# Order of the seven products in a Strassen-like feed-forward, and where the last layer norm's first row tiles are worked

## The chip, the cores and the metric

One core of one Trainium2 chip. The metric is the device time of one execution in microseconds (us). TensorE (PE) multiplies, VectorE (DVE), ScalarE (ACT) and GpSimd (POOL) work element by element, and SyncE (SP) issues most transfers.

## The reference

Two layers over 512 tokens of width 1024, in float32. The first mixes tokens with a state-space model, the second with attention. After each mixer and after each feed-forward part the sum with the input is normalised. The change touches the second layer's feed-forward and its norm, the last thing that is computed:

```python
def sq_relu_mlp(h, w1, w2):                       # w1 1024x4096, w2 4096x1024
    return jnp.square(jax.nn.relu(h @ w1)) @ w2

def layer_norm(x, g, b):
    mu = jnp.mean(x, axis=-1, keepdims=True)
    var = jnp.mean(jnp.square(x - mu), axis=-1, keepdims=True)
    return (x - mu) * lax.rsqrt(var + LN_EPS) * g + b

h = layer_norm(DN_ALPHA * h + sq_relu_mlp(h, w_ff1[1], w_ff2[1]), ln_ffn_g[1], ln_ffn_b[1])
```

## The kernel before

**Float32 as two parts.** Each operand of a matmul is cut into a rounded part and a remainder (`hi` and `lo`, float32r), and a product is three matmuls: hi x hi, lo x hi, hi x lo. For activations and weights alike ACT rounds (a copy into `hi`) and DVE subtracts (`lo`). In tile names `fh`, `fl` are the parts of hidden activations, `whi`, `wlo` those of a weight block.

**Weight blocks.** `ahead` loads 1 MB blocks in a fixed order on SP's queue into two `raw` buffers and splits them into three pairs of `whi`/`wlo` (L541 ACT, L543 DVE, the latter in two halves). A load waits until the split two blocks earlier has freed its buffer; block k + 3 is loaded as block k's product begins, and block k + 2 is split after the first half of product k.

**The last feed-forward, `feed_forward_rows`.** It runs in four quarters q of 1024 hidden units. A quarter first forms its hidden units in eight blocks of 128 units x 512 tokens (`dense`, L608 to L610; the first quarter has one weight unit of the four here, the rest earlier), then multiplies them with its part of `w2`. Two blocks form a pair, handled by `Pairs.add`: ACT takes relu and square into `sq`. With a block p and then q, cut into token halves, the second multiplication is done as a two by two scheme of seven products instead of eight (Strassen's, in a form with the sums p - q, `inner`, and `one`, made for the four pairs of a quarter). DVE forms these sums, and for each ACT rounds and DVE subtracts. `fo` holds the two parts of `one`, which only product 1 reads. Products 3 and 4 read a block itself (`hi[0]`, first and second half), 2 and 5 the difference `out`, 6 and 7 `in`.

**The products.** `SEVEN` lists in which order they are done and to which parts of the result each is added. One product is 24 matmuls: two row halves t = 0, 1, four pairs each, three matmuls (L886 to L888) per pair. The result stays in SBUF as row tiles 0 to 3 of 128 tokens x 1024, each as two `z` tiles of 128x512; DVE adds each product to them from PSUM (L976). A product's entry (r, n, sign) stands for row tile 2r + t and column half n. Row tiles 0 and 1 get additions from products 1, 3, 4, 5 and 7 only; products 2 and 6 go to row tiles 2 and 3 alone.

`w2` is combined in the same way: a block is plain, or the sum of two (16 such sums are made ahead in DRAM by a copy on SP's queue and an adding DMA on GpSimd's, L566 and L568), or a difference. A difference is loaded as two blocks and subtracted by DVE (L555) before it is split. `BLOCKS` lists this per product, in the order of `SEVEN`.

**The end.** In the last quarter products 2 and 6 are done for t = 0 first and then for t = 1. `norm(t)` works on DVE with one square root on ACT: two `bn_stats`, the root's reciprocal, then for each half a subtraction of the mean with the scale `g` (L923, L930) and a multiply-add with `b` into `o` (L932), stored by SP (L933). The norms of row tiles 0 and 1 run after product 2 of t = 0, that of tile 2 after product 2 of t = 1, that of tile 3 at the end. All order within `feed_forward_rows` is as written (a manual schedule); each engine runs its instructions in that order.

Of the kernel before, what the change touches and what calls it, by code (L numbers as in the profile page):

```python
# [9 lines left out]
F32 = mybir.dt.float32  # L10
F32R = mybir.dt.float32r
I32 = mybir.dt.int32
AF = mybir.ActivationFunctionType
ALU = mybir.AluOpType
# [3 lines left out]
DM = 1024  # L18
# [58 lines left out]
class Net:  # L77
# [590 lines left out]
    class Norm:  # L668
# [43 lines left out]
        def root(self):  # L712
            next(self.r)
# [130 lines left out]
    class Pairs:  # L844
# [4 lines left out]
        def add(self, ps):  # L849
            net, nc, v = self.net, self.net.nc, self.net.nc.vector  # L850
            first, second = slice(0, T // 2), slice(T // 2, T)
            x = net.f("sq")
            nc.scalar.activation(x, ps, AF.Relu)
            nc.scalar.activation(x, x, AF.Square)
            if self.p is None:
                self.p = x
                self.hi, self.lo = [[net.f(n, dt=F32R) for _ in range(3)] for n in ("fh", "fl")]
                self.one = net.f("fo", dt=F32R)
                self.inner = net.f("in")
                v.tensor_tensor(self.inner[:, first], x[:, second], x[:, first], op=ALU.subtract)  # L860
                nc.scalar.copy(self.hi[0][:, first], x[:, first])
                v.tensor_tensor(self.lo[0][:, first], x[:, first], self.hi[0][:, first].bitcast(F32), op=ALU.subtract)
                return
            p, q, hi, lo, one, inner = self.p, x, self.hi, self.lo, self.one, self.inner
            self.p = self.inner = None
            outer = net.f("out")
            v.tensor_tensor(outer, p, q, op=ALU.subtract)
            nc.scalar.copy(hi[1], outer)
            v.tensor_tensor(inner[:, second], q[:, first], q[:, second], op=ALU.subtract)
            nc.scalar.copy(hi[2], inner)  # L870
            v.tensor_tensor(p[:, first], p[:, first], q[:, second], op=ALU.subtract)
            nc.scalar.copy(one[:, first], p[:, first])
            nc.scalar.copy(hi[0][:, second], q[:, second])
            v.tensor_tensor(lo[1], outer, hi[1].bitcast(F32), op=ALU.subtract)
            v.tensor_tensor(lo[2], inner, hi[2].bitcast(F32), op=ALU.subtract)
            v.tensor_tensor(one[:, second], p[:, first], one[:, first].bitcast(F32), op=ALU.subtract)
            v.tensor_tensor(lo[0][:, second], q[:, second], hi[0][:, second].bitcast(F32), op=ALU.subtract)
            cut = lambda i, c: (hi[i][:, c], lo[i][:, c])
            self.out.append({1: (one[:, first], one[:, second]), 2: cut(1, second), 3: cut(0, first), 4: cut(0, second),
                             5: cut(1, first), 6: cut(2, first), 7: cut(2, second)})  # L880

    def mm3_rows(self, ps, a, tok, w, k, start, stop):
# [5 lines left out]
        pe.matmul(ps, ahi[:, tok], wlo[:, k, :], start=False, stop=stop)  # L888


    SEVEN = ((1, ((0, 0, 1), (1, 1, 1))), (3, ((0, 1, 1), (1, 1, 1))), (7, ((0, 0, 1),)), (4, ((0, 0, 1), (1, 0, 1))),
             (5, ((0, 0, 1), (0, 1, -1))), (2, ((1, 0, 1), (1, 1, -1))), (6, ((1, 1, 1),)))

    def feed_forward_rows(self, u0, h, act, pairs, rows, out):

        nc, v, pe = self.nc, self.nc.vector, self.nc.tensor
        toks = [slice(128 * t, 128 * t + 128) for t in range(4)]
        z = [[None, None] for _ in toks]
        g, b = [], []
# [9 lines left out]
                    nc.scalar.mul(z[t][n], ps, ALPHA)  # L909
                    yield  # L910

        def norm(t):

            self.n += 1
            st = self.small.tile([128, 16], F32, tag="st", name=f"st{self.n}")
            mu, var, s, y, r = [st[:, i:i + 1] for i in (12, 13, 14, 15, 0)]
            yield v.bn_stats(st[:, 0:6], z[t][0])
            v.bn_stats(st[:, 6:12], z[t][1])
            v.bn_aggr(st[:, 12:14], st[:, 0:12])
            v.tensor_scalar(var, var, self.col(6), None, op0=ALU.add)  # L920
            nc.scalar.activation(s, var, AF.Sqrt)
            v.reciprocal(y, var)
            v.scalar_tensor_tensor(z[t][0], z[t][0], mu, g[0], op0=ALU.subtract, op1=ALU.mult)  # L923

            v.scalar_tensor_tensor(y, s, 0.5, y, op0=ALU.mult, op1=ALU.mult)
            v.reciprocal(r, s)
            v.scalar_tensor_tensor(y, r, 0.5, y, op0=ALU.mult, op1=ALU.add)
            for n in range(2):
                if n:
                    v.scalar_tensor_tensor(z[t][n], z[t][n], mu, g[n], op0=ALU.subtract, op1=ALU.mult)  # L930
                o = self.f("o")
                v.scalar_tensor_tensor(o, z[t][n], y, b[n], op0=ALU.mult, op1=ALU.add)  # L932
                nc.sync.dma_start(out=out[toks[t], 512 * n:512 * n + 512], in_=o)  # L933

        N, first = 11, 4

        def start(i):
            self.ahead(u0 + i + 4, 0)

        def middle(i):  # L940
            self.ahead(0, u0 + i + 3)

        with self.tc.manual_schedule():
            turn = turned()
            self.ahead(0, u0 + 5)
            for q in range(4):
                last = q == 3
# [13 lines left out]
                if last:  # L961
                    for i, x in enumerate((g, b)):
                        for n in range(2):
                            x.append(self.f("gb", pool=self.B))
                            nc.sync.dma_start(out=x[n], in_=rows[i:i + 1, 512 * n:512 * n + 512].to_broadcast([128, 512]))
                left, todo, ws = pairs.out, [], {}
                pairs.out = []

# [8 lines left out]

                for i, (m, outs) in enumerate(self.SEVEN[0:5 if last else 7]):
                    at = N * q + first + i
                    start(at)  # L980
                    ws[m] = self.split_t.pop(u0 + at)
                    for t in range(2):
                        product(m, t, outs)
                        if t == 0:
                            middle(at)
                        if last and m == 5:
                            todo.append(norm(t))
            self.n += 1
            pre = self.small.tile([128, 1], F32, tag="pre", name=f"pre{self.n}")
            nc.scalar.activation(pre, left[0][3][0][:, 0:1].bitcast(F32), AF.Sqrt, bias=self.col(6), scale=0.0)  # L990
            for m in (2, 6):
                ws[m] = self.split_t.pop(u0 + 3 * N + first + (5 if m == 2 else 6))
            for t in range(2):
                for m, outs in self.SEVEN[5:7]:
                    product(m, t, outs)
                    if m == 2:
                        for c in todo:
                            for _ in c:
                                pass
                        todo = [norm(2 + t)]  # L1000
                        next(todo[0])
            for _ in todo[0]:
                pass

    def boundary(self, u, src, settle, z, g, b, follow, pool=None, begun=None):

# [411 lines left out]
FILL = {26: 4, 29: 2, 30: 4, 31: 1, 33: 1, 35: 2}  # L1418
UNITS = dict(glu=8, w_out=4, ff0=32, kvq=3, att=8, wo=4)

BLOCKS = ((0, 3, ALU.subtract), (1, 3, ALU.add), (2, 3, ALU.add), (2, 0, ALU.add), (3,), (0,), (0, 1, ALU.add))


@with_exitstack
def net_kernel(ctx, tc, a):
# [14 lines left out]
    for q in range(4):  # L1440
        for i in range(11):
            src = [a["ff1"][8 * q + j].rearrange("p k n -> p (k n)") for j in range(8)]
            if i < 4:
                units.append((src[i], (8, 256), 0))
                continue
            c = BLOCKS[i - 4]
            if len(c) > 1 and c[2] == ALU.add:
# [126 lines left out]
```

## Time and profile before

| | |
|---|---|
| median of three runs | 1190.16 us (1188.77 to 1190.49) |
| profiled execution, its own time | 1187.36 us |
| its span, first to last instruction | 1185.6 us |
| TensorE busy | 1136.3 us, 96% |
| DVE, ACT, GpSimd busy | 66%, 47%, 2% |
| mean granted TensorE clock | 0.991 of full |

A share is an average over stages: what an edit is worth is read where it stands, from what the engine that sets the end waits for.

### The profile page before, as it was taken

The numbers are of one execution on the slowest core, as the hardware profiler recorded it, in microseconds if no ns is written. First come the engines' busy times: TensorE is split into PE (matmuls) and PEld (weight loads), VectorE is DVE, ScalarE is ACT, GpSimd is POOL, SyncE is SP. The second block draws the span as 40 slices with busy tenths as digits, with TensorE's granted clock in tenths as the row PEclk, the third lists the DMA queues.
The fourth block names the chain that finished last, engine by engine and source line by source line (L and its number), as shares of the span: only waits on it lengthen the run. The fifth ranks groups of instructions, "written<-read, shape, count | busy, mean of one in ns | idle before, by whom it ended". The sixth has DMA issues, their size and how long they took to land.

```text
span 1185.6 us, 15947 instructions
## 1 busy us (share of the span) xinstructions
PE 1136.3 (96%) x6384; PEld 972.7 (82%) x6384; DVE 787.2 (66%) x1397; ACT 558.5 (47%) x939; POOL 20.2 (2%) x30
## 2 busy tenths in 40 slices
PE   5899999999999999999999999999999999999993
PEld 3778788899888888888899779989978878878872
DVE  8999552477454433433576788868887676676688
ACT  4888551337413413313436666634773643643540
POOL 0000000000011101000000000000000000000000
PEclk9999999999999999999999999999999999999997
DMA  4123261223699999722321012221335344344431
GB/s 169 40 91 95 89 222 71 72 72 108 187 282 269 293 325 247 215 107 72 107 72 45 32 59 90 72 72 40 116 135 210 114 154 159 142 142 165 155 142 71
DMA packets 39722, 157.54 MB, mean 133 GB/s; under 512 B 11456, under 2 KB 11584, under 8 KB 26720
## 3 DMA queue, kind: packets, MB, share of 16 engines
q1 hardware_dynamic: 30048, 137.64, 32.2%
q0 software_dynamic: 8448, 16.78, 8.0%
q10 hardware_dynamic: 1152, 2.10, 0.5%
q8 instruction: 50, 0.82, 0.3%
q14 instruction: 24, 0.20, 0.1%
HBM read 152.31 MB, written 37.75 MB: 160 GB/s over the span
## 4 chain that ended last, share of the span: by engine, by line
PE 85%; DVE 10%; ACT 4%; issue 1%; DMA 0%
PE ps L610 21%; PE ps L609 21%; PE ps L608 21%; PE ps L887 4%; PE ps L888 4%; PE ps L886 4%; PE ps L397 1%; PE ps L396 1%; PE ps L315 1%; PE ps L380 1%; PE ps L1329 1%; PE ps L642 1%; PE ps L352 1%; DVE wlo L543 1%; DVE tmpw L264 1%
## 5 line engine op out<-in xcount | busy, mean ns | idle before, releaser
L541 ACT CAST whi<-raw 128x2048 fp32r<-128x2048 f32 (+1 forms) x99 | 181.8, 1843 | 173.5 <-DMA raw<-in_ff 112.3
L543 DVE TENSOR_TENSOR wlo<-raw,whi 128x1024 fp32r<-128x1024 f32 (+1 forms) x198 | 225.5, 1179 | 37.6 <-ACT whi L541 37.6
L608 PE MATMUL ps<-hh,whi 128*128 128x512 f32 (+1 forms) x704 | 244.6, 347 | 0.0
L609 PE MATMUL ps<-hl,whi 128*128 128x512 f32 (+1 forms) x704 | 243.4, 346 | 0.0
L610 PE MATMUL ps<-hh,wlo 128*128 128x512 f32 (+1 forms) x704 | 243.3, 346 | 0.0
L609 PEld LDWEIGHTS ps<-hl,whi 128*128 128x128 f32 x704 | 133.3, 189 | 16.3
L610 PEld LDWEIGHTS ps<-hh,wlo 128*128 128x128 f32 x704 | 133.3, 189 | 16.3
L608 PEld LDWEIGHTS ps<-hh,whi 128*128 128x128 f32 x704 | 133.3, 189 | 16.2
L608 PE MATMUL ps<-fh,whi 128*128 128x512 f32 (+1 forms) x304 | 108.4, 357 | 0.0
L609 PE MATMUL ps<-fl,whi 128*128 128x512 f32 (+1 forms) x304 | 108.1, 355 | 0.0
L610 PE MATMUL ps<-fh,wlo 128*128 128x512 f32 (+1 forms) x304 | 108.1, 355 | 0.0
L796 ACT ACTIVATE relu<-ps 128x512 f32<-128x512 f32 x32 | 19.0, 595 | 127.7 <-PE ps L610 127.7
L798 DVE TENSOR_TENSOR relu<-relu 128x512 f32<-128x512 f32 x32 | 22.1, 691 | 84.3 <-ACT fh L797 84.3
L976 DVE TENSOR_TENSOR z<-z,ps 128x512 f32<-128x512 f32 x96 | 62.0, 682 | 22.1 <-PE ps L888 21.7
L886 PE MATMUL ps<-whi,fh 128*128 128x512 f32 x192 | 74.7, 389 | 0.0
L888 PE MATMUL ps<-wlo,fh 128*128 128x512 f32 x192 | 74.7, 389 | 0.0
L887 PE MATMUL ps<-whi,fl 128*128 128x512 f32 x192 | 74.7, 389 | 0.0
L609 PEld LDWEIGHTS ps<-fl,whi 128*128 128x128 f32 x304 | 57.4, 189 | 8.2
L610 PEld LDWEIGHTS ps<-fh,wlo 128*128 128x128 f32 x304 | 57.4, 189 | 8.2
L608 PEld LDWEIGHTS ps<-fh,whi 128*128 128x128 f32 x304 | 57.4, 189 | 8.1
L814 DVE TENSOR_TENSOR z<-z,ps 128x512 f32<-128x512 f32 (+1 forms) x30 | 17.4, 579 | 55.8 <-PE ps L610 55.8
L608 PE MATMUL ps<-yh,whi 128*128 128x512 f32 x128 | 52.3, 410 | 0.0
(302 smaller groups left out, 2207.9 us busy)
## 6 DMA issues: line engine op xcount, KB each, us to landing
raw<-in_ff SPq DMA_DIRECT2D x64, 1024.0 KB, 4.8
sum<-in_ff POOLq DMA_DIRECT2D x16, 1024.0 KB, 13.3
raw<-sum SPq DMA_DIRECT2D x16, 1024.0 KB, 4.8
raw<-in_glu SPq DMA_DIRECT2D x8, 1024.0 KB, 5.7
raw<-in_w_out SPq DMA_DIRECT2D x4, 1024.0 KB, 4.8
raw<-in_wo SPq DMA_DIRECT2D x4, 1024.0 KB, 4.7
raw<-in_kvq SPq DMA_DIRECT2D x3, 1024.0 KB, 4.8
raw<-in_attq SPq DMA_DIRECT2D x4, 576.0 KB, 3.6
```

The source lines that it names most:

```text
L541: self.nc.scalar.copy(hi, raw)
L543: self.put_off(lambda c=c: self.nc.vector.tensor_tensor(lo[:, c], raw[:, c], hi[:, c].bitcast(F32), op=ALU.subtract))
L608: pe.matmul(ps, whi, ahi, start=start, stop=False)
L609: pe.matmul(ps, whi, alo, start=False, stop=False)
L610: pe.matmul(ps, wlo, ahi, start=False, stop=stop)
L796: self.nc.scalar.activation(r, ps, AF.Relu)
L798: self.nc.vector.tensor_tensor(r, r, r, op=ALU.mult)
L814: v.tensor_tensor(z[m][:, tok], z[m][:, tok], ps, op=ALU.add)
L886: pe.matmul(ps, ahi[:, tok], whi[:, k, :], start=start, stop=False)
L887: pe.matmul(ps, alo[:, tok], whi[:, k, :], start=False, stop=False)
L888: pe.matmul(ps, ahi[:, tok], wlo[:, k, :], start=False, stop=stop)
L976: v.tensor_tensor(x, x, ps, op=ALU.add if sign > 0 else ALU.subtract)
```

## The change

The seven products are done in the order 3, 4, 5, 7, 1, 2, 6 instead of 1, 3, 7, 4, 5, 2, 6, and the weight blocks follow, so that the difference (two loads) stands at place five instead of one. `Pairs.add` makes the second half of `hi[0]`, `lo[0]` first instead of last. In the last quarter row tiles 0 and 1 are complete after the fifth product, and their norms (`norm_early`) begin there: ACT takes sums, squares and the scaling, DVE the steps of one element per row; the factor `g` is multiplied by GpSimd for tile 0 and by DVE for tile 1. For tiles 0 to 2 the offset `b` is first written to `out` by one DMA of 384 rows, and the rest is added to it by DMAs of GpSimd's queue; tile 2's last scaling goes to ACT. Tile 3 is as before.

```diff
@@ Pairs.add
             outer = net.f("out")
+            nc.scalar.copy(hi[0][:, second], q[:, second])
             v.tensor_tensor(outer, p, q, op=ALU.subtract)
+            v.tensor_tensor(lo[0][:, second], q[:, second], hi[0][:, second].bitcast(F32), op=ALU.subtract)
             nc.scalar.copy(hi[1], outer)
...
             nc.scalar.copy(one[:, first], p[:, first])
-            nc.scalar.copy(hi[0][:, second], q[:, second])
...
             v.tensor_tensor(one[:, second], p[:, first], one[:, first].bitcast(F32), op=ALU.subtract)
-            v.tensor_tensor(lo[0][:, second], q[:, second], hi[0][:, second].bitcast(F32), op=ALU.subtract)
@@ order
-    SEVEN = ((1, ((0, 0, 1), (1, 1, 1))), (3, ((0, 1, 1), (1, 1, 1))), (7, ((0, 0, 1),)), (4, ((0, 0, 1), (1, 0, 1))),
-             (5, ((0, 0, 1), (0, 1, -1))), (2, ((1, 0, 1), (1, 1, -1))), (6, ((1, 1, 1),)))
+    SEVEN = ((3, ((0, 1, 1), (1, 1, 1))), (4, ((0, 0, 1), (1, 0, 1))), (5, ((0, 0, 1), (0, 1, -1))), (7, ((0, 0, 1),)),
+             (1, ((0, 0, 1), (1, 1, 1))), (2, ((1, 0, 1), (1, 1, -1))), (6, ((1, 1, 1),)))
-BLOCKS = ((0, 3, ALU.subtract), (1, 3, ALU.add), (2, 3, ALU.add), (2, 0, ALU.add), (3,), (0,), (0, 1, ALU.add))
+BLOCKS = ((1, 3, ALU.add), (2, 0, ALU.add), (3,), (2, 3, ALU.add), (0, 3, ALU.subtract), (0,), (0, 1, ALU.add))
@@ feed_forward_rows: the norms
+        def root(var, s, y, r):
             nc.scalar.activation(s, var, AF.Sqrt)
             v.reciprocal(y, var)
+            yield v.scalar_tensor_tensor(y, s, 0.5, y, op0=ALU.mult, op1=ALU.mult)
+            v.reciprocal(r, s)
+            v.scalar_tensor_tensor(y, r, 0.5, y, op0=ALU.mult, op1=ALU.add)
+        def norm_early(t):
+            st, (nm, var, s, y, r) = stats(t)
+            o = [self.f("o") for _ in range(2)]
+            for n in range(2):
+                nc.scalar.activation(o[n], z[t][n], AF.Identity, accum_out=st[:, 1 + n:2 + n])
+            yield
+            v.tensor_tensor(nm, st[:, 1:2], st[:, 2:3], op=ALU.add)
+            v.tensor_scalar(nm, nm, -1.0 / DM, None, op0=ALU.mult)
+            for n in range(2):
+                nc.scalar.activation(o[n], z[t][n], AF.Square, bias=nm, accum_out=st[:, 3 + n:4 + n])
+            yield
+            v.tensor_tensor(var, st[:, 3:4], st[:, 4:5], op=ALU.add)
+            v.tensor_scalar(var, var, 1.0 / DM, self.col(6), op0=ALU.mult, op1=ALU.add)
+            for _ in root(var, s, y, r):
+                pass
+            v.tensor_tensor(nm, nm, y, op=ALU.mult)
+            for n in range(2):
+                nc.scalar.activation(o[n], z[t][n], AF.Identity, bias=nm, scale=y)
+            yield
+            for n in range(2):
+                (nc.gpsimd if t == 0 else v).tensor_tensor(o[n], o[n], g[n], op=ALU.mult)
+                nc.gpsimd.dma_start(out=out[toks[t], 512 * n:512 * n + 512], in_=o[n], accum_op=ALU.add)
-        def norm(t):
+        def norm(t, late):
...
+            for _ in root(var, s, y, r):
+                v.scalar_tensor_tensor(z[t][0], z[t][0], mu, g[0], op0=ALU.subtract, op1=ALU.mult)
...
                 o = self.f("o")
+                if late:
+                    v.scalar_tensor_tensor(o, z[t][n], y, b[n], op0=ALU.mult, op1=ALU.add)
+                    nc.sync.dma_start(out=out[toks[t], 512 * n:512 * n + 512], in_=o)
+                else:
+                    nc.scalar.mul(o, z[t][n], y)
+                    nc.gpsimd.dma_start(out=out[toks[t], 512 * n:512 * n + 512], in_=o, accum_op=ALU.add)
@@ feed_forward_rows: the last quarter, after the loads of g and b
+                    nc.sync.dma_start(out=out[0:384, :], in_=rows[1:2, :].to_broadcast([384, DM]))
...
-                        if last and m == 5:
-                            todo.append(norm(t))
+                        if last and m == 1:
+                            todo.append(norm_early(t))
+                            for c in todo:
+                                next(c)
...
+            n0, n1 = todo
+            n2, n3 = norm(2, False), norm(3, True)
+            between = {(0, 2): (n0, n1), (0, 6): (n0, n1, n2), (1, 2): (n1, n2, n3), (1, 6): (n3,)}
             for t in range(2):
                 for m, outs in self.SEVEN[5:7]:
                     product(m, t, outs)
-                    if m == 2:
-                        for c in todo:
-                            for _ in c:
-                                pass
-                        todo = [norm(2 + t)]
-                        next(todo[0])
-            for _ in todo[0]:
-                pass
+                    for c in between[t, m]:
+                        next(c, None)
```

Three places of the programs. First TensorE at the start of the last quarter's products, right behind the hidden units. Before, the first two pairs of product 1:
```order
L886 MATMUL ps_9845<-whi_9701,fo_9522 128x512
L887 MATMUL ps_9845<-whi_9701,fo_9522 128x512
L888 MATMUL ps_9845<-wlo_9702,fo_9522 128x512
L886 MATMUL ps_9845<-whi_9701,fo_9610 128x512
L887 MATMUL ps_9845<-whi_9701,fo_9610 128x512
```
Now, the first two pairs of product 3:
```order
L886 MATMUL ps_9841<-whi_9699,fh_9516 128x512
L887 MATMUL ps_9841<-whi_9699,fl_9519 128x512
L888 MATMUL ps_9841<-wlo_9700,fh_9516 128x512
L886 MATMUL ps_9841<-whi_9699,fh_9602 128x512
L887 MATMUL ps_9841<-whi_9699,fl_9605 128x512
```
What stood on `fo` now stands on `fh` and `fl`, the first token halves of the blocks.

Second DVE after product 2 of t = 0 in the last quarter (line numbers grow by 35 or so in the changed kernel; `st` holds a row tile's statistics). Before, two additions to row tile 2, then the norm of tile 0 (`z_7932` and `z_8000`), of which the second half's passes and then all of tile 1's norm follow:
```order
L976 TENSOR_TENSOR z_7986<-z_7986,ps_10026 128x512
L976 TENSOR_TENSOR z_8014<-z_8014,ps_10026 128x512
L917 BN_STATS st_10041<-z_7932 128x6
L918 BN_STATS st_10041<-z_8000 128x6
L919 BN_AGGR st_10041<-st_10041 128x2
L920 TENSOR_SCALAR st_10041<-st_10041,c 128x1
L922 RECIPROCAL st_10041<-st_10041 128x1
L923 SCALAR_TENSOR_TENSOR z_7932<-z_7932,st_10041,gb_9835 128x512
L925 SCALAR_TENSOR_TENSOR st_10041<-st_10041 128x1
L926 RECIPROCAL st_10041<-st_10041 128x1
L927 SCALAR_TENSOR_TENSOR st_10041<-st_10041 128x1
L932 SCALAR_TENSOR_TENSOR o_10052<-z_7932,st_10041,gb_9839 128x512
```
Now:
```order
L1011 TENSOR_TENSOR z_7981<-z_7981,ps_10041 128x512
L1011 TENSOR_TENSOR z_8009<-z_8009,ps_10041 128x512
L937 TENSOR_TENSOR st_10010<-st_10010 128x1
L938 TENSOR_SCALAR st_10010<-st_10010,c 128x1
L920 RECIPROCAL st_10010<-st_10010 128x1
L921 SCALAR_TENSOR_TENSOR st_10010<-st_10010 128x1
L922 RECIPROCAL st_10010<-st_10010 128x1
L923 SCALAR_TENSOR_TENSOR st_10010<-st_10010 128x1
L941 TENSOR_TENSOR st_10010<-st_10010 128x1
L932 TENSOR_TENSOR st_10034<-st_10034 128x1
L933 TENSOR_SCALAR st_10034<-st_10034 128x1
```
The passes over 128x512 tiles are gone from between; steps of one element per row are left, each group behind ACT's passes.

Third ACT at the end, from the split of product 6's block on. Before, one square root for each of the four norms:
```order
L541 CAST whi_10004<-raw_9952 128x2048
L990 ACTIVATE pre_10024<-fh_9516,c 128x1
L921 ACTIVATE st_10041<-st_10041 128x1
L921 ACTIVATE st_10059<-st_10059 128x1
L921 ACTIVATE st_10077<-st_10077 128x1
L921 ACTIVATE st_10124<-st_10124 128x1
```
Now (the first dozen; tile 1's scaling, tile 2's root, two scalings of tile 2 and tile 3's root follow):
```order
L541 CAST whi_10005<-raw_9955 128x2048
L930 ACTIVATE o_10011,st_10010<-z_7927 128x512
L930 ACTIVATE o_10012,st_10010<-z_7995 128x512
L935 ACTIVATE o_10011,st_10010<-z_7927,st_10010 128x512
L935 ACTIVATE o_10012,st_10010<-z_7995,st_10010 128x512
L930 ACTIVATE o_10035,st_10034<-z_7934 128x512
L930 ACTIVATE o_10036,st_10034<-z_8002 128x512
L1027 ACTIVATE pre_10039<-fh_9516,c 128x1
L919 ACTIVATE st_10010<-st_10010 128x1
L943 ACTIVATE o_10011<-z_7927,st_10010 128x512
L943 ACTIVATE o_10012<-z_7995,st_10010 128x512
L935 ACTIVATE o_10035,st_10034<-z_7934,st_10034 128x512
```
Tile 0 is `o_10011` and `o_10012`, tile 1 `o_10035` and `o_10036`; L930 takes sums, L935 squares, L943 scales. The passes of the two tiles interleave, and the root of tile 0 stands behind the sums of tile 1.

On GpSimd, which had no instruction after 627 us, there now follow a library reload, and in the end two multiplications and six adding DMAs in the order of the tiles. On SP's queue the write of 384 rows of `out` stands behind the four loads of `g` and `b`, ahead of the load of the fourth product's block.

## Rows read from the trace of the kernel before

**Rows 1.** The page: busy us, share and instructions of each engine.
```profile
PE 1136.3 (96%) x6384; PEld 972.7 (82%) x6384; DVE 787.2 (66%) x1397; ACT 558.5 (47%) x939; POOL 20.2 (2%) x30
```

**Rows 2.** Timeline, last quarter's first product: start us, duration us, [idle before].
```profile
1125.60 0.39 PE L886 MATMUL ps<-whi,fo 128*128 128x512 f32 x1
1127.09 0.69 DVE L867 TENSOR_TENSOR out<-sq,sq 128x512 f32<-128x512 f32 x1 [0.83 <-ACT sq L854]
1128.86 0.40 ACT L872 CAST fo<-sq 128x256 fp32r<-128x256 f32 x1
1129.31 0.50 PE L886 MATMUL ps<-whi,fo 128*128 128x512 f32 x1 [1.52 <-ACT fo L872]
1133.45 0.39 PE L886 MATMUL ps<-whi,fh 128*128 128x512 f32 x1
```

**Rows 3.** Timeline: first matmuls of products one and two, quarters 1-3.
```profile
872.44 0.48 PE L886 MATMUL ps<-whi,fo 128*128 128x512 f32 x1
879.77 0.39 PE L886 MATMUL ps<-whi,fh 128*128 128x512 f32 x1
955.93 0.39 PE L886 MATMUL ps<-whi,fo 128*128 128x512 f32 x1
963.79 0.39 PE L886 MATMUL ps<-whi,fh 128*128 128x512 f32 x1
1039.95 0.39 PE L886 MATMUL ps<-whi,fo 128*128 128x512 f32 x1
1049.41 0.40 PE L886 MATMUL ps<-whi,fh 128*128 128x512 f32 x1
```

**Rows 4.** Windows, third quarter: busy PE PEld DVE ACT POOL, PEclk, DMA, GB/s.
```profile
1046.00:1048.00 2.00, 2.00 (x6) 1.59 (x5) 2.00 (x3) 0.00 (x0) 0.00 (x0) 0.51 0.00 0
```

**Rows 5.** Timeline of DVE over the norms at the end.
```profile
1158.13 1.29 DVE L976 TENSOR_TENSOR z<-z,ps 128x512 f32<-128x512 f32 x2 [0.69 <-PE ps L888]
1160.65 0.21 DVE L919 BATCH_NORM_AGGREGATE st<-st 128x2 f32<-128x12 f32 x1
1162.33 0.75 DVE L932 SCALAR_TENSOR_TENSOR o<-z,st,gb 128x512 f32<-128x512 f32 x1
1169.56 0.69 DVE L917 BATCH_NORM_STATS2 st<-z 128x6 f32<-128x512 f32 x1
1181.62 0.75 DVE L932 SCALAR_TENSOR_TENSOR o<-z,st,gb 128x512 f32<-128x512 f32 x1
```

**Rows 6.** Block loads: a pair's landing, DVE's subtraction, ACT's cast.
```profile
DMA to landing us min/median/max: 4.7/5.8/6.8
1111.55 2.36 DVE L555 TENSOR_TENSOR raw<-raw,raw 128x1024 f32<-128x1024 f32 x2
L541 ACT CAST whi<-raw 128x2048 fp32r<-128x2048 f32 (+1 forms) x99 | 181.8, 1843 | 173.5 <-DMA raw<-in_ff 112.3
```

**Rows 7.** Windows while `gb` loads move; DMA issues, DRAM copies.
```profile
1123.00:1124.00 1.00, 1.00 (x6) 0.82 (x5) 0.10 (x1) 0.86 (x1) 0.00 (x0) 1.00 0.95 367
1124.00:1125.00 1.00, 1.00 (x6) 0.83 (x5) 1.00 (x1) 0.00 (x0) 0.00 (x0) 1.00 0.09 35
sum<-in_ff SPq DMA_DIRECT2D x16, 9.5
```

**Rows 8.** Lines: ACT's square of 128x512, its accumulator's read.
```profile
L854 ACT ACTIVATE sq<-sq 128x512 f32<-128x512 f32 x32 | 20.2, 632 | 1.0
L1309 ACT ACTIVATION_READ_ACCUMULATOR p<-ps,sst 128x1 f32 x32 | 6.3, 196 | 0.0
```

**Rows 9.** GpSimd: lines; its DMA queue; adding DMAs, us to landing.
```profile
L242 POOL MEMSET TT<- 128x1024 f32 x2 | 1.8, 954 | 0.0
L568 POOL DMA_DIRECT2D sum<-in_ff x16 | 16.6, 1038 | 461.3 <-DMA sum<-in_ff 461.3
q0 software_dynamic: 8448, 16.78, 8.0%
sum<-in_ff POOLq DMA_DIRECT2D x16, 1024.0 KB, 13.3
```

More of the change, by code (lines that the diff above doesn't have):

```diff
@@ L910, in turned, with stats @@
                     yield
-        def norm(t):
+        def stats(t):
             self.n += 1
             st = self.small.tile([128, 16], F32, tag="st", name=f"st{self.n}")
-            mu, var, s, y, r = [st[:, i:i + 1] for i in (12, 13, 14, 15, 0)]
+            return st, [st[:, i:i + 1] for i in (12, 13, 14, 15, 0)]
+        def root(var, s, y, r):
+            nc.scalar.activation(s, var, AF.Sqrt)
+            v.reciprocal(y, var)
+            yield v.scalar_tensor_tensor(y, s, 0.5, y, op0=ALU.mult, op1=ALU.mult)
[24 more added lines that the diff above has]
+        def norm(t, late):
+            st, (mu, var, s, y, r) = stats(t)
             yield v.bn_stats(st[:, 0:6], z[t][0])
@@ L920, in norm @@
             v.tensor_scalar(var, var, self.col(6), None, op0=ALU.add)
[L921 to L927, printed above, removed]
+            for _ in root(var, s, y, r):
+                v.scalar_tensor_tensor(z[t][0], z[t][0], mu, g[0], op0=ALU.subtract, op1=ALU.mult)
             for n in range(2):
@@ L931, in norm @@
                 o = self.f("o")
-                v.scalar_tensor_tensor(o, z[t][n], y, b[n], op0=ALU.mult, op1=ALU.add)
-                nc.sync.dma_start(out=out[toks[t], 512 * n:512 * n + 512], in_=o)
+                if late:
[4 more added lines that the diff above has]
+                    nc.gpsimd.dma_start(out=out[toks[t], 512 * n:512 * n + 512], in_=o, accum_op=ALU.add)
         N, first = 11, 4
```

## Prediction

> **What bounds the kernel now.** The page comes first: TensorE is busy for 96% of the span [rows 1], so only two kinds of time can be won, gaps in its work and the time after its last matmul. I looked for the gaps with the waits of TensorE over the last layer: there are two waits at the start of each quarter's products and no other. The timeline of the last quarter shows why [rows 2]. Call the start of its products T = 0 (1125.60). Product 1 reads `fo`, the last thing that the last pair makes: the square is ready just before 1127.09, DVE forms `out`, `in` and p - q, ACT rounds two tiles, and `fo` only then, at 1128.86. TensorE, which has run nine matmuls on older pairs by then, waits 1.52 us for it, and a little more for DVE's remainder. The second product starts at 1133.45, 7.85 us after the first. Without a gap a product is 24 matmuls at about 0.227 us, 5.44 us, so this start costs 2.4 us. The same two rows for the other quarters [rows 3] give 7.33, 7.86 and 9.46 us: 1.9, 2.4 and 4.0 us lost. The third is dearer since the granted clock stands at 0.51 for some 3 us after the gap [rows 4], the level of 1.2 GHz: 6 matmuls in 2 us where the full clock gives 9.
>
> The end is bound by DVE. From 1158.13 (T+32.5) it has work without a pause to 1182.37 (T+56.8) [rows 5], long after TensorE's last matmul. The span ends 3.2 us after DVE, with the last output transfer.
>
> **The starts.** Product 3, now first, reads the first token halves of `fh` and `fl`, made when the first block of each pair came, 5 us earlier. Product 4, due at T+5.44, reads the second halves. In the new `add` ACT rounds them first: square ready at T+1.45, copy 0.40, DVE's `out` to 2.1, `fl` at T+2.5: 2.9 us to spare. Products 5 and 7 need tiles that exist by T+4.3 and start at T+10.9 and T+16.3; `fo` has until T+21.8. No start should wait. Gain in the first three quarters: 1.9 + 2.4 + 4.0 = 8.3 us. The 2.4 us of the last are inside the end's sum, below.
>
> **The weights.** The block made of two loads and a DVE subtraction moves from position one of a quarter, where DVE had the slack of the matmuls on `act`, to position five. In the last quarter I laid the DVE and transfer rows end to end: pair work to T+4.6, two updates (0.6 each, [rows 5]) to 5.8, the split of product 5's block to 8.1, at 2.36 for a DVE pass over a block [rows 6]. That frees the buffer for the two loads; a pair lands 4.7 and 6.8 us after issue [rows 6], T+15. The subtraction, ACT's casts and the remainders, two such passes, are done at about T+20.4, and product 1 wants them from T+21.8: 1.4 us to spare. DVE is late by then with three updates, and the block of product 6 is loaded at T+20.4, lands 4.7 us later, is cast in 1.84 [rows 6] by 27.1 and split by 29.5, its first half by 28.3; the matmul that reads that half stands at T+30.4. So the chain stays hidden, by 1.4 to 2 us. If that cover is gone, each us of it is a us of time.
>
> **The prefill of `out`.** 1.5 MB from DRAM to DRAM, put on SP's queue behind the four `gb` loads. Those fill the DMA engines to T-1 and then leave them [rows 7]. The `gb` rows are the nearest: broadcast lines of the same tensor, 367 GB/s. By them it takes 4.3 us, 5.3 with some loss, and is over by T+4.5. Behind it waits only the load of product 7's block, 1 MB, which then lands by about T+8, when ACT asks for it (the middle of product 4, T+8.2). Price zero. The other bound is the row of DRAM copies, 9.5 us for 1 MB [rows 7], 14 us for this one: then that load lands at about T+16.5, when its product is due at 16.3. Its cast and split make TensorE wait and the two loads behind it wait too; laid out the same way it moves the end by 6 us. Those 9.5 us were measured amid other loads and adding DMAs; I take 4.3 to 5.3, as the tensor and the broadcast are the same.
>
> **The norms.** DVE loses the two norms of row tiles 0 and 1 and the last multiply-add of tile 2. ACT gets, for each of the two, four passes with accumulation or a square (0.63 [rows 8], 0.53 from one to the next, and 0.20 for the accumulator's read [rows 8]) and two scalings. In order:
> DVE ends the split at T+29.5 and updates tiles 1 and 3 to 30.8; tile 0's mean is at 31.1. ACT: its squares 31.2 to 32.7, tile 1's sums to 34.2, the early `Sqrt`, tile 0's root at 34.5, its scaling to 36.4, tile 1's squares to 37.8. DVE waits for ACT here, 3.4 us in three pieces. Tile 1's root takes it from 37.9 to 39.1 (the steps of one element are 0.08 to 0.25 us apart; all those of a norm fill 1160.65 to 1162.33 less one 0.67 us pass [rows 5]). From there DVE has no pause. Tiles 2 and 3 took it from 1169.56 to 1182.37, 12.8 us [rows 5]; it now does two multiplies for tile 1 more (1.2), two of the 0.75 us passes less (1.4), one update less, done earlier (0.6), and waits some 0.4 because the root no longer hides behind the subtraction: 12.4 us. DVE ends at T+51.5 instead of 56.8: 5.3 us gained, of which 2.4 are the start's.
>
> GpSimd's part must not end last. Tile 0's multiplies start at T+35.9. Its nearest compute row is a memset of twice the elements, 0.95 us [rows 9]; with two reads I take 1.2, between 0.5 and 2.4. Each adding DMA holds it 1.04 us [rows 9]. The last is issued at T+46.4, when tile 2 is scaled. Its 256 KB are 8 packets of 2 KB for each of 16 engines; the queue's row gives 0.08 x 16 x 1185.6 / 8448 = 0.18 us a packet [rows 9], 1.4 us. With about 2.4 us of start and receipt it lands by T+51, DVE's own last store by T+53.5. Slack of GpSimd: 6 us or so, counting its idle time before tile 2. Price zero, with the two bounds for the multiply as well.
>
> **Sum.** 8.3 + 5.3 = 13.6 us, against the profiled execution's 1187.36: 1173.8. That execution lies 2.8 us under the median of the three runs, 1190.16; taken from the median it is 1176.6, and I say 1176.5. The clock's dip need not fall on the same starts in every run: without it the gain is 12.0 (1178.2), with it at all four 18 or so (1172).
>
> **A rule against it.** No row shows GpSimd's first computing instruction; only memsets and DMA issues stand there. The Trainium skill (GPSIMD Engine Reference, Instruction dispatch) says that the first call to a freshly loaded kernel pays about 6 us that no instruction in the profile shows, and the changed program does have a library reload ahead of the first multiply. By it GpSimd uses up its slack and the end moves by an estimated 1.2 us, to 1177.7. The Trainium skill (SBUF — State Buffer, Who interferes with whom) also says that a VectorE instruction with two SBUF inputs and a GpSimd instruction that reads SBUF block each other for a whole instruction; no run here shows it yet, and by it tile 1's root could wait for one multiply, an estimated 0.7 us.
>
> **The rivals.**
> A, GpSimd ends last. For it: the page gives 13.3 us to landing for an adding DMA of 1 MB [rows 9], a quarter of that is 3.3 and not 1.4. Six in series from T+37.1 with 2 us of start would land at T+59, 5.4 us late: 1182. A first multiply that comes x us late costs about x - 5, so that 6 us late gives 1177.5 and 10 us 1181.5. Against it: those were timed behind the plain copy of the same block, and the packets of the queue say 1.4. Chance 0.14, 1177.5 to 1182.
> B, the weight chain shows through: the prefill at the slow row's rate, or the moved pair landing later than its row. Up to 6 us: 1178 to 1182.6. Against it: both rows that are like it are fast. Chance 0.10.
> C, the change does not do what it says at the starts: the first product still waits for the pair, or its block is not split. Then the last start's 2.4 us stay as well, and of the end's 5.3 us only 2.9 are won: 1187.3. The order of the halves speaks against it. Chance 0.02.
> D, slower. The last adding DMA lands after T+60 + 8.3, where the span ended counted with the earlier starts. That takes more than 4.7 us for each of the six in series; at the 13.3 us of the 1 MB row they would end at T+119, 51 us too late, about 1241. It would have to be three times what the packets say. Chance 0.04, and 0.03 for a GpSimd that is late by just so much that nothing is won, 1188 to 1192.
>
> **How the numbers follow.** The forecast has 0.67, and 1176.5 is its time, 1173 to 1179 by the clock and the small waits. What a measurement of this kernel can tell is about 0.2%, 2.4 us. The range takes in the forecast, A and B: 1173 to 1182.5. Faster: the forecast, A and B, 0.91; the same, with C at the edge, 0.05; slower 0.04.
>
> **What would show it.** TensorE has no wait over 0.3 us at the start of products, and the second product starts 5.4 us after the first in every quarter; no clock of 0.5 there. In the last quarter no wait of TensorE for `whi` or `wlo`; DVE idle for about 3.4 us before tile 1's root, then busy for 12 us to some 51.5 us after the start of the products. The chain that ended last closes with DVE and a store of SP. It is wrong if the chain closes with an adding DMA or GpSimd (A or D), if TensorE waits for ACT's casts near the fifth product (B), or if `fo` still stands in its waits (C).

## The result, and the profile of the changed kernel

The changed kernel takes 1177.51 us (median of 4 runs, 1176.74 to 1180.09), the kernel before 1189.49 us on the same chip: a ratio of 0.9903, 95% interval 0.9884 to 0.9921. Forecast: 1176.5.

The profiled execution took 1178.21 us, its span is 1176.3 us (before: 1185.6). TensorE's share is as before [rows 1]:

```profile
PE 1132.7 (96%) x6384; PEld 973.0 (83%) x6384; DVE 779.1 (66%) x1391; ACT 571.1 (49%) x961; POOL 28.1 (2%) x38
```

**The starts.** The timeline of TensorE, with the first matmuls of products one and two of the third and the last quarter, is to be read against [rows 2] and [rows 3]:

```profile
1037.11 0.39 PE L886 MATMUL ps<-whi,fh 128*128 128x512 f32 x1
1042.55 0.39 PE L886 MATMUL ps<-whi,fh 128*128 128x512 f32 x1
...
1118.71 0.39 PE L886 MATMUL ps<-whi,fh 128*128 128x512 f32 x1
1124.15 0.39 PE L886 MATMUL ps<-whi,fh 128*128 128x512 f32 x1
```

5.44 us from product one to product two: no start waits any more, and the list of TensorE's waits over the last feed-forward (from 835 us to the end) is empty. (Ahead of it, in the last layer's attention, TensorE waits 0.9 us for ACT and DVE in both kernels.) From one quarter's first product to the next it is 81.6 to 81.7 us, where before it was 83.5, 84.0 and 85.7 [rows 2, 3]: 8.3 us won. The windows show the clock of the third quarter (the last three numbers are granted clock, DMA share and GB/s), which stood at 0.51 before [rows 4], and one of two low stretches (652 to 656 and 662 to 667 us) in the attention part, which the change does not touch:

```profile
654.00:656.00 2.00, 2.00 (x11) 2.00 (x10) 0.00 (x0) 1.76 (x3) 0.00 (x0) 0.50 0.00 0
1046.00:1048.00 2.00, 2.00 (x11) 1.65 (x10) 2.00 (x4) 0.00 (x0) 0.00 (x0) 1.00 0.83 221
```

Such low stretches come and go from run to run, 0 to 2 in the attention part in these profiles, and three profiles have one more near 52 us. The profile of before had one, this one has two, and so the first quarter's products begin 1.4 us later (873.81 against 872.44). Over the profiles of this document these products begin at 870.7 us with no low stretch ahead, at 872.4 with one, near 873.8 with two and near 875.5 with three, some 1.6 us for each (the run with the fetch moved, which starts late, left out). Executions of one kernel lie 1.7 to 6.4 us apart, so I compare the ends below from T, the first matmul of the last quarter's products (here 1118.71).

**The end.** VectorE gained 2.6 us and not 5.3: it ends at T+54.1 (before T+56.8, forecast T+51.5). The span ends at T+57.6 (before T+60.0), 2.4 us earlier. With the 8.3 us of the starts, less the 1.4 us of the low stretch, that is the 9.3 us between the two spans. VectorE's timeline shows what it did instead; a bracket is the idle time before an instruction and who ended it:

```profile
1147.02 2.36 DVE L543 TENSOR_TENSOR wlo<-raw,whi 128x1024 fp32r<-128x1024 f32 x2 [2.08 <-ACT whi L541]
...
1152.47 0.16 DVE L937 TENSOR_TENSOR st<-st 128x1 f32<-128x1 f32 x1 [0.46 <-ACT o L935]
...
1153.98 0.16 DVE L921 SCALAR_TENSOR_TENSOR st<-st 128x1 f32<-128x1 f32 x1 [0.90 <-ACT st L919]
...
1157.66 1.84 DVE L937 TENSOR_TENSOR st<-st 128x1 f32<-128x1 f32 x1 [2.21 <-ACT o L935]
1159.54 0.21 DVE L938 TENSOR_SCALAR st<-st,c 128x1 f32<-128x1 f32 x1
...
1172.10 0.75 DVE L963 SCALAR_TENSOR_TENSOR o<-z,st,gb 128x512 f32<-128x512 f32 x1
```

Two things are new. The same sum of two 128x1 columns takes 0.16 us for tile 0 and 1.84 us for tile 1. It ends at 1159.50, and GpSimd's timeline has its second multiply end at 1159.48 (its start there, 0.2 us behind the step's, is rough, as all times of GpSimd are):

```profile
1155.65 1.29 POOL L946 TENSOR_TENSOR o<-o,gb 128x512 f32<-128x512 f32 x1 [527.77 <-ACT o L943]
1157.24 0.94 POOL L947 DMA_DIRECT2D out<-o  x1 [0.30 <-POOL o L946]
1157.88 1.60 POOL L946 TENSOR_TENSOR o<-o,gb 128x512 f32<-128x512 f32 x1
```

And the split of product 6's block begins at T+28.3, its end is T+30.7 where the forecast had 29.5. That block's load is issued at 1139.11, T+20.4, as forecast, but the DMA view of its window has it land 5.9 us later, beside one packet of an instruction queue (16 KB):

```profile
q1 hardware_dynamic: 144, 1.05, 46.2%
q8 instruction: 1, 0.02, 1.4%
...
raw<-sum SPq DMA_DIRECT2D x1, 1024.0 KB, 5.9
```

The chain that ended last goes through both, in order of time:

```profile
1136.72 2.37 DVE wlo L558 x2
1139.11 5.87 DMA raw<-sum
1145.07 1.92 ACT whi L541
1150.92 1.52 ACT o L935 x4
1156.22 1.42 ACT o L935 x4
1157.66 1.85 DVE st L937
```

### The profile page after: what moved, and what is told of

It is laid out like the page before. It is cut to its first block, busy times and chain, and to the rows that moved or that the text cites. A ratio compares the mean times of both kernels' runs of the same rounds, so it can differ in the third digit from the quotient of the medians.

```text
span 1176.3 us, 15955 instructions
## 1 busy us (share of the span) xinstructions
PE 1132.7 (96%) x6384; PEld 973.0 (83%) x6384; DVE 779.1 (66%) x1391; ACT 571.1 (49%) x961; POOL 28.1 (2%) x38
## 4 chain that ended last, share of the span: by engine, by line
PE 87%; DVE 7%; ACT 3%; DMA 2%; issue 1%; SPq 0%; ACTq 0%; DVEq 0%
PE ps L609 23%; PE ps L610 23%; PE ps L608 22%; PE ps L886 3%; PE ps L888 3%; PE ps L887 3%; PE ps L397 1%; PE ps L396 1%; PE ps L315 1%; DMA raw<-in_glu 1%; PE ps L380 1%; PE ps L1363 1%; PE ps L642 1%; DMA raw<-in_ff 1%; PE ps L352 1%
## 5 line engine op out<-in xcount | busy, mean ns | idle before, releaser
L814 DVE TENSOR_TENSOR z<-z,ps 128x512 f32<-128x512 f32 (+1 forms) x30 | 17.3, 578 | 55.8 <-PE ps L610 55.8
```

The source lines that it names most:

```text
L814: v.tensor_tensor(z[m][:, tok], z[m][:, tok], ps, op=ALU.add)
```

## The experiments

Theory: the order of the products gives the starts and the norms give the end, as forecast; the 2.6 us that VectorE's end lacks are GpSimd's multiply holding VectorE's small step (1.7) and the instruction fetch delaying the load (1.1). Rivals: the order made the whole gain; the step or the load are late for other reasons.

A ratio is to the kernel before on the same chip, where it took 1188.69 to 1190.28 us.

| kernel | median us | ratio to before, 95% | VectorE's end, T+ | span's end, T+ |
|---|---|---|---|---|
| changed kernel | 1177.51 | 0.9903 [0.9884, 0.9921] | 54.1 | 57.6 |
| order alone | 1180.07 | 0.9905 [0.9891, 0.9920] | 55.9 | 59.2 |
| norms alone | 1188.16 | 0.9979 [0.9970, 0.9988] | 55.8 | 59.3 |
| tile 0's multiplies on VectorE | 1174.81 | 0.9871 [0.9857, 0.9886] | 52.8 | 55.8 |
| one-input steps | 1178.84 | 0.9897 [0.9881, 0.9913] | 53.5 | 57.0 |
| both tiles on GpSimd | 1179.73 | 0.9920 [0.9900, 0.9941] | 54.7 | 58.1 |
| fetch moved | 1184.26 | 0.9958 [0.9943, 0.9973] | 53.1 | 56.6 |
| prefill twice | 1185.93 | 0.9971 [0.9957, 0.9985] | 62.7 | 66.0 |
| pairs split as before | 1177.60 | 0.9905 [0.9883, 0.9927] | 54.1 | 57.6 |
| changed kernel again | 1179.07 | 0.9915 [0.9899, 0.9931] | 54.2 | 57.6 |
| VectorE's order changed too | 1175.79 | 0.9886 [0.9866, 0.9907] | 52.0 | 55.0 |
| that, and fetch moved | 1174.54 | 0.9875 [0.9854, 0.9895] | 50.7 | 53.9 |

**The order alone.**
```
 # kernel before, with:
-SEVEN = 1, 3, 7, 4, 5, 2, 6        BLOCKS, Pairs.add: as before
+SEVEN = 3, 4, 5, 7, 1, 2, 6        BLOCKS, Pairs.add: as changed
-                        if last and m == 5:
+                        if last and m == 1:
```


> The kernel before with the new order of the seven products, of the blocks and of the pairs' split alone; the norms stay on VectorE. Theory (the order and the norms are two separate gains, the order's lies in the starts): the starts of the four quarters lose their waits, 8.3 us up to the last quarter's first product; at the end VectorE stays the engine that ends last, its work begins about 1.5 us earlier against the first product than in the kernel before, so about 9.8 us in all: 1179.7 us where the kernel before has 1189.5. Rival (the end's gain came from the order too, the norms moved off VectorE gave nothing): the whole 12 us, 1177.5. Rival (the starts' waits are only passed on to later products): under 3 us, above 1186.


10.2 us under the kernel before of the same chip (1190.28). No wait of TensorE is left in the last feed-forward and the quarters are 81.6 to 81.7 us apart: the starts come from the order. At the end it gave 0.8 us, half of what was expected: here too the last block's load lands after 5.9 us beside the fetch. By the medians alone this version cannot be told from the changed kernel (0.9905 against 0.9903, and 0.9915 in its second measurement), so the times don't refute the rival that the order made the whole gain. The traces do: against T the changed kernel's VectorE ends 1.8 us earlier than here and its span 1.6 us. How much of that comes from the norms of tiles 0 and 1 and how much from tile 2's scaling on ACT was not separated.

**The norms alone.**
```
 # changed kernel, with SEVEN, BLOCKS, Pairs.add and the trigger (m == 5) of before
```


> The changed kernel with the old order of products, blocks and split; only the norms are moved to ScalarE and GpSimd. Theory: the waits at the four starts come back (8.3 us, with the low clock after the third or fourth), and at the end VectorE would end 4.5 us earlier against the first product than in the kernel before, less the 1.7 us in which GpSimd's multiply holds VectorE's small step and up to 1.1 us of a late block: a gain of 1.7 to 2.8 us, 1186.7 to 1187.8 us. Rival (the norms moved give nothing): 1189.5. Rival (the norms moved give what was predicted for the end, and what was lost came from the new order): 4.5 us or more, 1185 or less.


2.1 us, inside the expected span, but not for the expected reasons alone: against T the end gains only 0.7 us in this profile, VectorE's 1.0. The load of product 6's block is not late here, it lands after 4.9 us. The waits of TensorE (us in total, times, longest) are back:
```profile
PE ps L886 <- ACT fo L872: 5.4, 4, 1.5
PE ps L887 <- DVE fo L876: 1.3, 4, 0.3
```
and after three of the four the clock falls, here after the second and the last:
```profile
962.00:964.00 2.00, 2.00 (x6) 1.52 (x5) 2.00 (x3) 0.00 (x0) 0.00 (x0) 0.50 0.00 0
...
1134.00:1136.00 2.00, 2.00 (x7) 1.54 (x7) 2.00 (x2) 0.00 (x0) 0.00 (x0) 0.60 0.44 184
```
The dip in the last quarter makes TensorE late, and VectorE waits for its products (the last three waits are 1.88, 0.69 and 0.43 us). So the norms moved are worth less while the start waits: the two edits are not quite independent. Quarters here are 83.5, 85.7 and 85.6 us apart, so the starts cost 10 us in this execution, 8.3 in the profiled one of before: how often the clock falls differs from run to run.

**Tile 0's multiplies on VectorE.**
```
-                (nc.gpsimd if t == 0 else v).tensor_tensor(o[n], o[n], g[n], op=ALU.mult)
+                v.tensor_tensor(o[n], o[n], g[n], op=ALU.mult)
```


> The changed kernel with tile 0's two multiplies by g on VectorE instead of GpSimd, so that GpSimd computes nothing in the last stretch and only issues the adding transfers. Theory (VectorE's 128x1 sum of two inputs took 1.84 us instead of 0.16 because GpSimd's multiply held the port that both share): that step is back at 0.16 us; the two multiplies (0.68 us each) lie in the 1.8 us for which VectorE waits for ScalarE there, so the end comes 1.3 to 1.7 us earlier, 1175.8 to 1176.2 us. Rival (the 1.84 us have another cause, such as ScalarE's late result): the step stays long and the time is the same or up to 1.2 us longer, 1177.5 to 1178.7.


```profile
1152.73 1.40 DVE L946 TENSOR_TENSOR o<-o,gb 128x512 f32<-128x512 f32 x2
1154.85 0.16 DVE L937 TENSOR_TENSOR st<-st 128x1 f32<-128x1 f32 x1 [0.72 <-ACT o L935]
```
The step is back at 0.16 us, the two multiplies lie in the wait for ScalarE, which falls from 2.21 to 0.72, and VectorE's end comes 1.4 us earlier against T, though the load of product 6's block took 6.2 us here and not 5.9. The median fell by 2.7 us. The profile of this run has no low clock in the attention part and begins its last quarter 3.1 us earlier; what the executions without a profile had was not seen.

**One-input steps.**
```
-            v.tensor_tensor(var, st[:, 3:4], st[:, 4:5], op=ALU.add)
+            v.tensor_scalar(var, st[:, 3:4], st[:, 4:5], None, op0=ALU.add)
 # likewise for nm (twice) and for the two steps of the root
```


> The changed kernel with the early norm's small 128x1 steps written with one tensor input and the second value as a per-partition scalar (five kinds of steps, also the two in the root that all norms share); GpSimd's multiplies stay. Theory (the block needs two tensor inputs): the 1.84 us step falls to 0.22 us, about 1.6 us less; the rewritten steps are about 0.06 us longer each, 1.1 us over all that lie on VectorE's path: 0.5 us less in all, 1177.0 us. Rival (any small step beside GpSimd's multiply is held, a scalar operand too): a step there stays over 1 us long and the time rises by about 1 us, 1178.6.


```profile
1155.16 0.21 DVE L937 TENSOR_SCALAR st<-st 128x1 f32<-128x1 f32 x1 [2.16 <-ACT o L935]
...
1155.93 0.21 DVE L921 TENSOR_SCALAR st<-st 128x1 f32<-128x1 f32 x1
```
GpSimd:
```profile
1155.37 1.60 POOL L946 TENSOR_TENSOR o<-o,gb 128x512 f32<-128x512 f32 x1
```
The multiply begins 0.2 us after the first of these steps, as it did in the changed kernel, and now does not hold it; the later steps with a scalar operand (L921, L923, L941) run in the midst of the multiply and take 0.21 us each. So it is the second tensor input that waits, a scalar operand does not. The end is 0.6 us earlier against T, with a load that took 6.2 us; the median, 1178.84, cannot tell it from none.

**Both tiles on GpSimd.**
```
-                (nc.gpsimd if t == 0 else v).tensor_tensor(o[n], o[n], g[n], op=ALU.mult)
+                nc.gpsimd.tensor_tensor(o[n], o[n], g[n], op=ALU.mult)
```


> The changed kernel with the multiplies by g of both early tiles on GpSimd (the changed kernel has tile 1's two on VectorE). Theory (VectorE's operations with two tensor inputs wait while GpSimd computes): VectorE is rid of 1.28 us, but is held twice more, for what is left of a GpSimd multiply each time, so it gains nothing or loses up to 1.5 us: 1177 to 1179 us, with single steps of 1 us or more beside GpSimd's multiplies. Rival (only the step of the changed kernel is held, by accident of its place): VectorE ends 1.2 us earlier, 1176.3 us. GpSimd's later adding transfers land before VectorE's last stores in both.


VectorE:
```profile
1159.81 1.84 DVE L937 TENSOR_TENSOR st<-st 128x1 f32<-128x1 f32 x1 [2.20 <-ACT o L935]
...
1163.35 1.27 DVE L1011 TENSOR_TENSOR z<-z,ps 128x512 f32<-128x512 f32 x2
1164.53 0.69 DVE L953 BATCH_NORM_STATS2 st<-z 128x6 f32<-128x512 f32 x1
...
1166.01 1.57 DVE L921 SCALAR_TENSOR_TENSOR st<-st 128x1 f32<-128x1 f32 x1
```
GpSimd, tile 1:
```profile
1163.82 1.26 POOL L946 TENSOR_TENSOR o<-o,gb 128x512 f32<-128x512 f32 x1 [1.01 <-ACT o L943]
...
1165.99 1.56 POOL L946 TENSOR_TENSOR o<-o,gb 128x512 f32<-128x512 f32 x1
```
A second small step is held, until the second of these multiplies ends. The first of them runs beside an update (one input in PSUM) and a statistics pass (one input), both of their usual length. VectorE has 1.28 us less to do and ends 0.6 us later. Of that, 0.4 us come from the load of product 6's block, which took 6.2 us here (the first held step begins at T+39.35 instead of T+38.95). From there on VectorE needs 15.4 us, in the changed kernel 15.2: the second block, 1.4 us, costs about as much as the work that was taken away.

**The fetch moved.**
```
+        for _ in range(64):          # in s5, before the first warm-up matmul
+            self.nc.tensor.matmul(acc[-1][:, 0:64], self.idr, self.idr[:, 0:64], start=True, stop=True)
```


> The changed kernel with 64 small matmuls added at the very start, where TensorE idles (their results are overwritten by the next warm-up matmul). They shift TensorE's instruction count by 128, half the distance of two instruction fetches, so that the fetch which now falls into the load of product 6's block comes about 14 us later, when no load runs. Theory (the load lands 5.9 us after its issue instead of 4.8 because one of the 16 DMA engines serves the 16 KB fetch meanwhile): the load lands after 4.8 to 4.9 us, the split of that block and all that VectorE does behind it come 1.0 to 1.3 us earlier, VectorE ends 53.0 us after the last quarter's first product instead of 54.15, the time falls by about 1.1 us, to 1176.4 us. Rival (the load is late for its place behind the pair's loads or the prefill): it still lands after 5.8 us or more and nothing changes from 54.15 us.


The load's own window, where no packet of the instruction queue is left:
```profile
q1 hardware_dynamic: 144, 1.05, 57.8%
issues: line engine op xcount, KB each, median us to landing
raw<-sum SPq DMA_DIRECT2D x1, 1024.0 KB, 4.8
```
4.8 us, and VectorE's end at T+53.1: 1.0 us, as the theory had it; the long step is still there, 1.83 us. The packet has come 15 us earlier against T (T+6.6 instead of T+21.4), not 14 us later as I had written. The median is no measure, since the 64 matmuls took 13.9 us where TensorE idled for 6, and all behind them came later.

**The prefill twice.**
```
                     nc.sync.dma_start(out=out[0:384, :], in_=rows[1:2, :].to_broadcast([384, DM]))
+                    nc.sync.dma_start(out=out[0:384, :], in_=rows[1:2, :].to_broadcast([384, DM]))
```


> The changed kernel with the prefill of the three row tiles issued twice, the second right behind the first (the same values again). Theory (the prefill is hidden, with some 9 us to spare at the block of product 7): its second copy takes another 7 us of all queues, the block of product 7 lands about 14.5 us after the last quarter's first product instead of 7.5, the chain behind it (cast, split, the pair's load and its add) shifts by 4 to 5 us and shows at the products 1 and 6: VectorE ends 4 to 5 us later, and the time is about 1182 us. Rival (the slack covers a second prefill too): the same time, 1177.5 us, and no wait of TensorE. Rival (the second copy takes less than the first, since nothing is queued ahead of it): 4 us more on the load, 1 to 2 us in the time.


Twice as dear as expected, and I had left a queue out. The second copy waits 11.0 us for the first (both write the same rows), on SP, and so the load of product 7's block behind it is issued at 1123.40 instead of 1119.44, and competes with the second copy as well: it lands after 12.6 us instead of 6.7. ScalarE gets the block at T+17.3 instead of 7.5, TensorE waits, and the clock falls:
```profile
PE ps L886 <- ACT whi L541: 3.4, 2, 2.7
...
1138.00:1140.00 2.00, 1.96 (x4) 1.15 (x5) 2.00 (x2) 0.00 (x0) 0.00 (x0) 0.50 0.66 279
```
A lateness of 9.8 us costs a first wait of 2.75 us, so some 7 us were to spare: the single prefill is hidden.

**Pairs split as before.**
```
 # Pairs.add: hi[0]'s and lo[0]'s second halves last again
```


> The changed kernel with the split of the pair back in its old order (the second halves of the plain block cast and subtracted last); products, blocks and norms as changed. Theory (what starts a quarter early is that its first product reads the first halves, which are split before the last pair): the second halves are needed only 5.4 us later by the second product and done by then, so the quarters stay 81.6 to 81.7 us apart and the time is 1177.5 us. Rival (the new order of the split carries part of the 8.3 us): TensorE waits again at the second product of each quarter, 0.2 us or more each, 1178.5 us or more.


Theory: no wait of TensorE, 81.6 to 81.7 us between the quarters, the end where it was. This part of the change is worth nothing that shows.

**Two versions built on it,** beside the changed kernel on one chip.
```
 # both: tile 0's multiplies on VectorE, and
-            between = {(0, 2): (n0, n1), (0, 6): (n0, n1, n2), (1, 2): (n1, n2, n3), (1, 6): (n3,)}
+            between = {(0, 2): (n0, n1), (0, 6): (n0, n2, n1), (1, 2): (n1, n2, n3), (1, 6): (n3,)}
 # the second: also 64 matmuls of 32 by 16, as in the run with the fetch moved
```


> The changed kernel itself, for a comparison on the same chip as the two versions built on it: 1177.5 us, VectorE's end 54.15 us after the last quarter's first product, the small step at 1.84 us and the load of product 6's block landing after 5.9 us, as in its first profile, since both follow from the order of the instructions.

> The changed kernel with tile 0's multiplies on VectorE (as in the run before) and tile 2's first statistics ahead of tile 1's last early steps, where VectorE waits 0.72 us for ScalarE's squares. Theory (VectorE's path ends last, so only what it does and waits for counts): the first half of the statistics, 0.60 us, goes into that wait; VectorE ends 52.2 us after the last quarter's first product instead of 52.8, the time is about 0.6 us below that of the run with the multiplies alone (1174.8), 1174.2 us. Rival (ScalarE's passes or the adding transfers end last now): no change against 1174.8 us.

> The same as the version with the changed order on VectorE, and besides 64 very small matmuls (32 by 16) at the start, where TensorE idles, which move the instruction fetch out of the load of product 6's block. Theory (three separate losses at the end: the held step 1.7 us, the wait that the statistics fill 0.6 us, the late load 1.2 us): VectorE ends about 51.0 us after the last quarter's first product, the time is 1173.0 us if the small matmuls stay within the first 5.9 us of idle time. Rival (the matmuls take longer than the idle time, as the larger ones did): the first quarter's product comes later by what they take beyond it, up to 3 us, and the time is 1174 to 1176 us though the end is short.


The changed kernel came out at 1179.07, with the same ends. Against T the versions do what was expected: the wait for the squares is filled (T+52.0), and the load lands after 4.8 us (T+50.7). The small matmuls fit, 3.6 us. In time they lie 3.3 and 4.5 us below the changed kernel of that chip, and only the second one's interval (to 0.9895) is clear of that kernel's (from 0.9899); 1.2 us between the two is within the scatter, and so is the first one against the version with the multiplies alone.

## Why the prediction was right, and where its sum was not

**The starts: right, 8.3 us forecast and measured**, with its mechanism (the run with the order alone). It counted one dip of the clock, as in the profile of before, and named 12.0 to 18 us in all for none to four dips; the norms-only run had three.

**The weights: right but for one term.** The pair's add ended, and product 6's load was issued, at T+20.4 as worked out; no wait of TensorE. The load was taken at 4.7 us, the least of its row (4.7/5.8/6.8), and took 5.9: the end lost 1.0 to 1.1 us by it, shown by moving the fetch.

**The prefill: right.** It landed 12.5 us after its issue at 1111.14, T+4.9, against T+4.5, and the block behind it was there at T+7.5 (forecast: 8).

**The norms: the mechanism right, the sum mis-sized.** The step that failed is "the steps of one element are 0.08 to 0.25 us apart": one of them was held by GpSimd, 1.84 us. The prediction named such a hold beforehand, priced it at 0.7 us and left it out of its sum. The waits for ScalarE came to 0.46 + 0.90 + 2.21 = 3.6 us (forecast 3.4), and from tile 1's root VectorE had 12.2 us of work (12.4). Held step 1.7 and late load 1.1 are the 2.6 us between T+51.5 and T+54.1, to 0.2.
Of the Trainium skill's two rules the one (SBUF — State Buffer, Who interferes with whom) is what happened: a VectorE instruction with two SBUF inputs and a GpSimd instruction that reads SBUF exclude each other for a whole instruction. The estimate from it was 0.7 us, the trace has 1.7, since the small step met the multiply at its start.
The Trainium skill's other rule (GPSIMD Engine Reference, Instruction dispatch, about 6 us for a first call) does not show in this trace: ScalarE ends the scaling at 1156.22 and GpSimd's first multiply, begun after the first half of it at 1155.65, takes 1.29 us.

**The rivals.** GpSimd does not end last: its last adding DMA is issued by 1168.94, the last store of VectorE's results follows 1172.85, and the six land after 4.0 us in the median. The prediction's two terms for one of them, 1.4 us of packets and 2.4 us of start and receipt, make 3.8; no row gave the 2.4. (For D the six would have needed 4.9 us each, 68.3 less 39.1 over six, and not 4.7.) The weight chain stays hidden, the first products no longer wait.

**Why the total fits better than its terms.** In part by luck. By the profiled executions the change gained 9.2 us (1187.36 to 1178.21), 4.4 less than the sum's 13.6; by the medians it gained 12.0 (1189.49 to 1177.51). The median of before lies 2.1 us above its profiled execution, that of the changed kernel 0.7 us below. The mean granted clock of each execution points the same way: 0.991 in the profiled one of before, but 0.986 to 0.990 in the seventeen executions of it that the first runs above are compared with, on the whole the lower the longer they took; 0.989 to 0.992 in the four of the changed kernel, 0.991 in the profiled one. The old starts cost more where the clock falls oftener, as in the norms-only run, which fits; where the clock fell in the executions without a profile was not seen, so this part stays argued.

## What to carry to other kernels

Put first what needs nothing from the last result: up to two fifths of a gap's price here was the low clock after it (1.6 of 4.0 us). Before work goes to GpSimd, look at what VectorE does meanwhile: a step with two SBUF inputs, even of one column, can wait for GpSimd's whole instruction (1.84 and 1.57 us here), and work moved into a wait that VectorE has anyway was cheaper than work moved off it. Where a span's end hangs on one load, look for the instruction fetches of that stretch.

## What the hardware showed beyond that

The page counts 50 packets of the instruction queue q8, 0.82 MB, and TensorE has 6384 weight loads and 6384 matmuls: one 16 KB packet for 255 of its instructions, 27 to 32 us apart in the last feed-forward. That they are TensorE's follows from the run with the fetch moved: 128 more of its instructions shifted them by 15 us. The load of product 6's block, 1 MB, lands after 5.7 to 6.2 us in the nine profiles where such a packet begins 0.9 to 2.8 us after the load's issue, and after 4.8 us in the two where none comes during it. In the two others, before and norms alone, one comes only 4.2 and 4.4 us after the issue, and the load lands after 4.8 and 4.9: so late a packet costs it nothing that shows. How the packet delays the load (one of the 16 DMA engines serving it meanwhile, as the theory had it) no view shows. The Trainium skill (Runtime: NRT & Kernel Launch, Instruction fetch mechanics) says that an engine fetches in blocks of 16 KiB, 256 instructions, and calls the cost mostly hidden: the size agrees, and here it was not hidden from the load beside it.
